# A depthwise convolution of 31 taps as 256 small matmuls with Toeplitz tap matrices

## The chip, the core and the metric

The kernel runs on one core of a Trainium2 chip. The core has five engines with a queue each: TensorE (PE, matmuls; its weight loads stand as PEld), VectorE (DVE), ScalarE (ACT), GpSimd (POOL) and SyncE (SP), which here issues the DMAs. A DMA is carried by up to 16 DMA engines. The metric is the device time of one execution in microseconds (us).

## The reference

Two encoder layers over 1024 tokens of width 1024. In each, one input projection feeds four token mixers of 256 columns; their outputs go through an output projection, then a residual layer norm, a SwiGLU feed-forward part and another residual layer norm. The mixers are a conformer convolution, a bidirectional S5 state space layer, a short gated convolution and differential attention. The change is about the first:

```
def conformer_conv(h, dw_w, dw_b, ln_g, ln_b):
    a, g = jnp.split(h, 2, axis=-1)
    z = a * jax.nn.sigmoid(g)
    z = depthwise_conv(z, dw_w) + dw_b      # 31 taps, centred, one filter per channel
    z = layer_norm(z, ln_g, ln_b)
    return jax.nn.silu(z)
```

So each of 256 channels is convolved along the 1024 tokens with its own 31 weights. Everything is float32.

## The kernel before

**Precision.** A wide product of the projections is done as three matmuls of split operands (high and low parts, in a reduced fp32 format, `mm3`): tiles `cg` (`chan_gemm`, channels on partitions), `tg` (`tok_gemm`, tokens on partitions), `up` and `dn` (feed-forward), `wo`. Transposes go through PE as plain fp32 matmuls against an identity (`tr`); such an fp32 matmul shows as two records in the trace.

**Order of the work.** The program is written stage by stage (`mixers_in`, attention, feed-forward), but a `Weaver` records every operation, with a modelled duration, and then builds one static order for all engines by list scheduling. The priority of an operation is its place in the program plus an offset from the table `SHIFT`, by function and layer; operations that may run on several engines are placed with the help of the table `PREF`. All instructions are emitted from one helper, so every line of the profile says L461, and tile names tell them apart. On the chip each engine follows its list strictly: an instruction that waits holds all behind it on its engine, and SP's DMA issues are such a list too.

**A layer.** `load_small` brings the small vectors (31 tap rows, biases, gains) into `chraw` (38 rows x 256), PE transposes them (`chps`) to channel-major `chp`. In layer 0 `s5_params` loads the S5 parameters into `s5b`, transposes them (`s5ps`, `s5cps`) and computes tables on DVE. `conf_a` and `conf_g` form z = a x sigmoid(g) in tile `conv`. The S5 layer runs as eight pairs of groups: `s5_pair_tables` builds tables (tiles `s5t`, in a ring of four, and `s5k`), `s5_pair` does matmuls (`s5v`, `s5y`, `s5wp`) and vector operations between them on DVE and POOL. The short convolution's products stand between the pairs.

**The convolution.** `conf_conv` works with channels on partitions, for each of two channel tiles. Even and odd tokens are separated; with sums and differences of them the 31 taps take 46 `scalar_tensor_tensor` operations of some 505 columns and one `tensor_scalar`, all on DVE, each reading and writing the PSUM tile `cacc`, so they form a chain:

```
dst[:, lo:hi] = src[:, lo+k:hi+k] * weight(k) + dst[:, lo:hi]
```

Then ACT copies `cacc` to `acc`, PE transposes that to tokens on partitions (`cvt`, 16 per layer), DVE takes mean and variance (`bn_stats`) and normalises into `cxn`, PE transposes back (`cvb`, 16), and ACT applies gain, bias and Silu and hands the result to the output projection by way of DRAM (`yT`). After that come the products for attention (`ktp`, `tg`) and the attention heads, whose first score tile is `sc`.

Of the kernel before, what the change touches and what calls it, by code (L numbers as in the profile page):

```python
# [9 lines left out]
F32 = mybir.dt.float32  # L10
# [8 lines left out]
P = 128  # L19
# [26 lines left out]
R_CW, R_SW, R_CB, R_LG, R_LB, R_GB, NROW, NCH = 0, 31, 34, 35, 36, 37, 38, 54  # L46
# [16 lines left out]
class Weaver:  # L63
# [3 lines left out]
    SHIFT = {"None": 315, "attn_finish0": 3482, "attn_finish1": -8000, "attn_heads0": 4301, "attn_heads1": 1337,  # L67
# [11 lines left out]
    PREF = {"attn_finish0 gpsimd": -5172, "attn_finish0 scalar": -2719, "attn_finish0 vector": -2311,  # L79
# [106 lines left out]
    def record(self, eng, method, args, kwargs):  # L186
# [104 lines left out]

    LAT = {"tensor": 200.0, "vector": 140.0, "scalar": 160.0, "gpsimd": 120.0, "sync": 100.0}

    def schedule(self):
# [44 lines left out]
        while True:  # L339
# [104 lines left out]
            for x in o.succ:  # L444
                x.left -= 1
                x.ready = max(x.ready, o.end + (0.0 if e == x.eng == "tensor" else self.LAT[e]))
                if x.left == 0:
                    offer(x)
# [26 lines left out]
class Trunk:  # L475
# [3 lines left out]
    def __init__(self, ctx, tc, t):  # L479
# [17 lines left out]
        self.mhalf = self.cp.tile([P, 4], F32, name="mhalf")  # L497
# [59 lines left out]
    def layer_norm(self, r, g, bb, dst=None, parts=1):  # L557

        nc = self.nc
        st = self.sp.tile([P, 2, 6], F32, tag="st", name=self.nm("st"))  # L560
# [79 lines left out]
    def load_small(self, l):  # L640
        nc, t = self.nc, self.t
        raw = self.wb([NROW, GW], "chraw")
        nc.sync.dma_start(raw[R_CW:R_CW + CONV_K, :], t["conf_dw_w"][l])
        nc.sync.dma_start(raw[R_SW:R_SW + 3, :], t["sc_conv_w"][l])
        for r, k in ((R_CB, "conf_dw_b"), (R_LG, "conf_ln_g"), (R_LB, "conf_ln_b"), (R_GB, "s5_b_glu")):
            nc.sync.dma_start(raw[r:r + 1, :], t[k][l:l + 1, :])
        ch = self.cp.tile([P, 2, NCH], F32, tag="chp", name=self.nm("chp"), bufs=1)
# [192 lines left out]
    def s5_ring(self):  # L840

        tabs = [self.S([P, SROW], F32, "s5t") for _ in range(2)]
        wk = self.S([P, SROW], F32, "s5k")
        self.s5t, self.s5w = [], []
        for i in range(4):
            T = tabs[i // 2][:, (i % 2) * 1856:(i % 2) * 1856 + 1856]
# [12 lines left out]
        self.s5BD = tabs[0][:, 3712:3904].rearrange("p (r g m) -> p r g m", r=2, g=2)  # L859
# [3 lines left out]
    def s5_pair_tables(self, pr):  # L863
# [3 lines left out]
        R, G = self.s5t[pr % 4], self.s5p  # L867
# [143 lines left out]
    def conv_alloc(self):  # L1011
        T = self.S([P, 2, 2, NJ, P], F32, "conv")
# [660 lines left out]
```

## Time and profile before

| | |
|---|---|
| median of three runs | 2543.04 us (2540.66 to 2545.26) |
| the profiled execution | 2556.47 us, span 2554.3 us, mean granted TensorE clock 0.959 |
| PE busy | 2342.5 us, 92% of the span |
| DVE busy | 1690.8 us, 66% |
| ACT, POOL busy | 777.7 us (30%), 1383.9 us (54%) |

The page gives busy times over the whole span; they are sums over stages with different limits. The stages, found from the first and last instructions of certain tiles, are: layer 0's mixers up to the first score tile at 350 us, its attention to 624, its feed-forward part to 1307; layer 1's mixers to 1607, attention to 1876, feed-forward to 2489, and the last norm. A wait's row names the instruction that waited, the one that ended the wait, the total, how often, and the longest. The granted clock is a share of 2.4 GHz: 0.5 is 1.2 GHz.

### The profile page before, as it was taken

The page shows a single profiled execution, that of the slowest core. Times are in us where ns is not written, and L with a number is a line of the kernel's source. Part 1 is how long each engine was busy: PE and PEld are TensorE (multiplying, and loading weights), DVE is VectorE, ACT ScalarE, POOL GpSimd, SP SyncE. Part 2 cuts the span into 40 slices and gives each one's busy share as a digit, 9 for nine tenths or more (in the row PEclk, how much of TensorE's full clock was granted, in tenths as well). Part 3 has the DMA queues.
Part 4 walks back from the last instruction along what each step waited for, and adds up shares of the span by engine and source line. Part 5 has one row for each costly group of instructions (what it writes and reads, how often), then busy time and mean ns, then how long its engine had stood idle before and what let it go on. Part 6 is the DMA issues. An engine that isn't in the chain of part 4 may idle for free. (4 is left out here: it accounts for less than half of the span.)

```text
span 2554.3 us, 32493 instructions
## 1 busy us (share of the span) xinstructions
PE 2342.5 (92%) x12412; PEld 1941.9 (76%) x12412; DVE 1690.8 (66%) x2584; ACT 777.7 (30%) x1333; POOL 1383.9 (54%) x1162
## 2 busy tenths in 40 slices
PE   7798698888999999999999996898889999999997
PEld 7677586776888788888787785777678888888885
DVE  6789867886555555555668897688755444554456
ACT  2210245553222222222222111656433222222231
POOL 1524364546666555566675252644476655555574
PEclk9998798999999999999999997999999999999998
DMA  5212111114111111111322121211131111111112
GB/s 134 77 36 75 42 58 61 62 58 145 56 50 50 51 57 58 50 50 50 108 94 60 30 96 41 73 63 60 65 132 53 55 58 50 58 50 50 58 50 99
DMA packets 126439, 167.59 MB, mean 66 GB/s; under 512 B 18432, under 2 KB 100940, under 8 KB 126028
## 3 DMA queue, kind: packets, MB, share of 16 engines
q1 hardware_dynamic: 126284, 165.52, 20.5%
q8 instruction: 98, 1.61, 0.3%
q14 instruction: 57, 0.47, 0.1%
HBM read 139.25 MB, written 26.25 MB: 65 GB/s over the span
## 5 line engine op out<-in xcount | busy, mean ns | idle before, releaser
L461 PE MATMUL up<-xT,wring 128*128 128x512 f32 x2112 | 485.9, 389 | 0.0
L461 PEld LDWEIGHTS up<-xT,wring 128*128 128x128 f32 x2112 | 396.4, 188 | 82.3
L461 PE MATMUL dn<-wring,g 128*128 128x512 f32 x1920 | 451.0, 391 | 7.8 <-POOL wring L461 6.5
L461 POOL TENSOR_TENSOR wring<-upraw,wring 128x512 fp32r<-128x512 f32 x220 | 307.6, 1401 | 257.1 <-ACT wring L461 255.0
L461 PEld LDWEIGHTS dn<-wring,g 128*128 128x128 f32 x1920 | 359.3, 188 | 88.2 <-POOL wring L461 10.6
L461 PE MATMUL up<-xB,wring 128*128 128x512 f32 x1584 | 371.8, 390 | 0.0
L461 PEld LDWEIGHTS up<-xB,wring 128*128 128x128 f32 x1584 | 298.4, 189 | 62.2 <-DVE xT L461 0.2
L461 DVE TENSOR_TENSOR r<-r,dn 128x512 f32<-128x512 f32 x288 | 197.5, 686 | 212.0 <-PE dn L461 212.0
L461 ACT CAST wring<-upraw 128x512 fp32r<-128x512 f32 x217 | 134.6, 621 | 459.1 <-PE dn L461 164.8
L461 PE MATMUL cg<-xh,win 128*128 128x512 f32 x640 | 211.7, 400 | 4.6 <-POOL win L461 3.2
L461 DVE TENSOR_REDUCE asm<-sc 128x1 f32<-128x1024 f32 x128 | 155.3, 1217 | 65.9 <-PE sc L461 64.8
L461 PE MATMUL tg<-win,xh 128*128 128x256 f32 x1024 | 196.4, 291 | 1.4 <-ACT vq L461 0.9
L461 PE MATMUL wo<-wout,yhl 128*128 128x512 f32 x768 | 195.7, 402 | 0.0
L461 PEld LDWEIGHTS tg<-win,xh 128*128 128x128 f32 x1024 | 165.6, 197 | 4.1 <-ACT vq L461 1.3
L461 ACT ACTIVATE probs<-sc,asm 128x1024 f32<-128x1024 f32 x128 | 143.6, 1123 | 82.1 <-DVE asm L461 81.9
L461 PEld LDWEIGHTS wo<-wout,yhl 128*128 128x128 f32 x768 | 143.5, 192 | 28.9
L461 POOL TENSOR_TENSOR wring<-w2raw,wring 128x512 fp32r<-128x512 f32 x80 | 102.7, 1288 | 106.5 <-ACT wring L461 106.4
L461 PE MATMUL tg<-win,xl 128*128 128x256 f32 x512 | 148.8, 291 | 0.0
L461 PEld LDWEIGHTS cg<-xh,win 128*128 128x128 f32 x640 | 121.0, 189 | 35.1 <-issue 4.6
L461 POOL TENSOR_TENSOR wring<-tw,wring 128x512 fp32r<-128x512 f32 x88 | 126.2, 1434 | 13.2 <-ACT wring L461 13.2
L461 PE MATMUL cg<-xl,win 128*128 128x512 f32 x320 | 125.5, 392 | 0.0
L461 DVE TENSOR_TENSOR tw<-tu,up 128x512 f32<-128x512 f32 x66 | 45.4, 687 | 107.5 <-PE up L461 107.2
(234 smaller groups left out, 3856.9 us busy)
## 6 DMA issues: line engine op xcount, KB each, us to landing
upraw<-in_w_ffn_dram SPq DMA_DIRECT2D x88, 512.0 KB
w2raw<-in_w_ffn_dram SPq DMA_DIRECT2D x44, 512.0 KB
wraw<-in_w_in_dram SPq DMA_DIRECT2D x36, 512.0 KB
woraw<-in_w_out_dram SPq DMA_DIRECT2D x16, 512.0 KB
r<-x_scr SPq DMA_DIRECT2D x16, 512.0 KB
x_scr<-xr SPq DMA_DIRECT2D x14, 512.0 KB
yt<-yT_scr SPq DMA_DIRECT2D x16, 384.0 KB
x1row<-x_scr SPq DMA_DIRECT2D x12, 512.0 KB
```

What stands on the lines that cost most here:

```text
L461: getattr(e, method)(*args, **kwargs)
```

## The change

The tap loops on DVE are replaced by matmuls. For a block of 96 outputs of one channel, a window of 128 inputs is needed (96 + 31 - 1, with padding). A 128 x 96 matrix that holds the channel's taps along its diagonals maps the window to the outputs. The 1024 tokens are cut into 11 such blocks, so the moving operand has 11 columns, one per block, and there is one matmul per channel: 256 per layer, plain fp32.

- `conv_table`, once at the start: the taps of both layers go into the zeroed tile `ctw`, are halved by POOL and written to a DRAM table `taps_scr`, in which each row serves nine channels. Two transfers write zeros at both ends of the rows (58 x 864 values) and two, one per layer, write the taps between, 31 x 29 runs of nine values.
- `conv_windows`: 22 transposes per layer (`cvw`) bring the padded z to windows with tokens on partitions (`convz`).
- `conv_part`, three per layer, placed ahead of S5 pairs 0, 3 and 6: for every nine channels one DMA reads a 128 x 864 tile from the table with overlapping rows (29 per layer, in a ring of three: `ctap` twice and a part of tile `conv`), then nine matmuls into PSUM tile `cvo`; six evacuations on DVE per layer add the bias.
- `conv_norm`: mean and variance over 96-token blocks, normalisation, 22 transposes `cvb` of 96 columns, Silu.

Beside it `load_small` no longer loads the taps (`chraw` has 6 rows), the S5 table ring has two tiles instead of four, `conf_g` computes tanh in place in PSUM, two small pools have one buffer less, the scheduler's model has a higher floor for fp32 matmuls (128 ns) and an extra 75 ns for results that go to PE, and all numbers of `SHIFT` and `PREF` are new, so that the whole order moves. The core of the diff:

```diff
-    SHIFT = {"None": 315, "attn_finish0": 3482, "attn_finish1": -8000, "attn_heads0": 4301, "attn_heads1": 1337,
...
+    SHIFT = {"None": -921, "attn_finish0": -1102, "attn_finish1": -4137, "attn_heads0": 3121, "attn_heads1": -3970,
...
-            return max(108.0, 0.4167 * 4 * n + 5) * (0.57 if pair else 1.0), 0
+            return max(128.0, 0.4167 * 4 * n + 5) * (0.57 if pair else 1.0), 0
...
+    def conv_table(self):
+
+        nc, t = self.nc, self.t
+        self.wrd = self.dp.tile([DEPTH * NCK, WROW], F32, name="taps_scr")
+        w = self.wb([P, CB * CG], "ctw")
+        nc.gpsimd.memset(w, 0.0)
+        taps = w[64:64 + CONV_K, 0:DEPTH * NCK * CG].rearrange("p (l c) -> p l c", l=DEPTH)
+        for l in range(DEPTH):
+            nc.sync.dma_start(taps[:, l, 0:GW], t["conf_dw_w"][l])
+
+        nc.gpsimd.tensor_scalar(taps, taps, 0.5, None, op0=ALU.mult)
+        lo, hi = CB * CG, (CWIN - 1) * CG
+        nc.sync.dma_start(self.wrd[:, 0:lo], w[0:DEPTH * NCK, :])
+        nc.sync.dma_start(self.wrd[:, hi:WROW], w[0:DEPTH * NCK, :])
+        for l in range(DEPTH):
+            nc.sync.dma_start(self.wrd[l * NCK:(l + 1) * NCK, lo:hi].rearrange("q (i k) -> i q k", k=CG),
+                              taps[:, l].rearrange("p (q k) -> p q k", k=CG))
...
-    def conf_conv(self, l, yT):
...
-            v.tensor_scalar(acc[:, 1], w, cw(NROW + 8), cw(R_CB), op0=ALU.mult, op1=ALU.add)
-            taps(acc[:, 1], w, lambda k: cw(NROW + 8 + k), None, [k for k in range(-8, 8) if k], H)
...
-            taps(acc[:, 0], e, lambda k: cw(R_CW + 15 + 2 * k), acc[:, 1], [0] + [k for k in range(-7, 8) if k], H)
-            taps(acc[:, 1], zf, lambda k: cw(R_CW + 14 + 2 * k), None, range(-7, 9), H + 1)
...
+    def conv_part(self, l, i):
+
+        nc = self.nc
+        ps = self.d((P, 2, 512), "cvo")
+        for h in range(2):
+            b = 2 * i + h
+            c0, c1 = b * CBANK, min(GW, b * CBANK + CBANK)
+            for c in range(c0, c1):
+                q, k = divmod(c, CG)
+                tap = self.tring[q % 3]
+                if k == 0:
+                    src = self.wrd[l * NCK + q:l * NCK + q + 1, :]
+                    nc.sync.dma_start(tap, bass.AP(src.tensor, src.offset, [[CG, CWIN], [1, CB * CG]]))
+                nc.tensor.matmul(ps[0:CB, h, (c - c0) * NBLK:(c - c0 + 1) * NBLK], lhsT=tap[:, k::CG], rhs=self.zT[:, :, c], start=True, stop=True)
+            nc.vector.tensor_tensor(self.zT[0:CB, :, c0:c1].rearrange("p b c -> p c b"),
+                                    ps[0:CB, h, 0:(c1 - c0) * NBLK].rearrange("p (c b) -> p c b", b=NBLK),
+                                    self.cbias[:, c0:c1].unsqueeze(2).to_broadcast([CB, c1 - c0, NBLK]), op=ALU.add)
...
+            if pr % 3 == 0:
+                self.conv_part(l, pr // 3)
             self.s5_pair(pr)
...
+        self.conv_norm(l, yT)
...
+        self.conv_table()
```

Where it moves the order, at three places. First SP's list near the program's start (`x` are the input tiles, `wraw` weight blocks), before:

```order
L461 DMA lam_287<-in_da_subln_g_dram 64x1 x2
L461 DMA lam_1253<-in_da_subln_g_dram 64x1
L461 DMA x_3_83<-in_x_dram 128x1024 x4
L461 DMA lam_1253<-in_da_subln_g_dram 64x1
L461 DMA wraw_108<-in_w_in_dram 128x4x256
L461 DMA wraw_109<-in_w_in_dram 128x4x256
L461 DMA s5b_124<-in_s_a_re_dram 16x2x64
L461 DMA s5b_124<-in_s_a_im_dram 16x2x64
```

and now:

```order
L470 DMA taps_scr<-ctw_89 31x29x9 x2
L470 DMA wraw_110<-in_w_in_dram 128x4x256
L470 DMA wraw_111<-in_w_in_dram 128x4x256
L470 DMA ctap_53_134<-taps_scr 128x864
L470 DMA ctap_54_135<-taps_scr 128x864
L470 DMA chraw_117<-in_sc_conv_w_dram 3x256
L470 DMA chraw_117<-in_conf_ln_g_dram 1x256
L470 DMA chraw_117<-in_conf_ln_b_dram 1x256
L470 DMA chraw_117<-in_s_b_glu_dram 1x256
L470 DMA conv_120<-taps_scr 128x864
L470 DMA s5b_126<-in_s_a_re_dram 16x2x64
```

The two taps transfers and the first three reads of the table stand between the last input tiles and the S5 parameters; `chraw` comes behind the table too.

Second, PE's list where the small vectors and S5 parameters are transposed, before:

```order
L461 MATMUL chps_117<-ident,chraw_115 128x38 x2
L461 MATMUL tg_112<-win_88,xl_6_86 128x256
L461 MATMUL tg_112<-win_88,xh_4_84 128x256 x2
L461 MATMUL tg_112<-win_88,xl_6_86 128x256
L461 MATMUL s5ps_125<-ident,s5b_124 128x16 x3
L461 MATMUL s5ps_125<-ident,s5b_124 16x16
L461 MATMUL s5ps_126<-ident,s5b_124 128x16 x3
L461 MATMUL s5ps_126<-ident,s5b_124 16x16
```

and now:

```order
L470 MATMUL tg_114<-win_90,xl_6_86 128x256
L470 MATMUL tg_114<-win_90,xh_4_84 128x256 x2
L470 MATMUL tg_114<-win_90,xl_6_86 128x256
L470 MATMUL tg_114<-win_90,xh_4_84 128x256
L470 MATMUL s5ps_127<-ident,s5b_126 128x16 x3
L470 MATMUL s5ps_127<-ident,s5b_126 16x16
L470 MATMUL tg_114<-win_90,xh_4_84 128x256
```

Now `chps` stands nine rows ahead of `s5ps`. Ahead of `s5ps` PE had 96 `tg` matmuls before and has 70 now, and the same 64 transposes of `x`.

Third, PE's list in layer 0 at the first S5 pair, where the taps are now (three ring tiles, nine matmuls each):

```order
L470 MATMUL cg_174<-xh_4_84,win_91 128x512
L470 MATMUL cvw_162<-ident,conv_120 128x128 x3
L470 MATMUL s5v_164<-s5u_112,s5t_144 64x128 x8
L470 MATMUL cvo_163<-convz_133,ctap_53_134 96x11 x9
L470 MATMUL cvo_163<-convz_133,ctap_54_135 96x11 x9
L470 MATMUL cvo_163<-convz_133,conv_120 96x11 x9
L470 MATMUL cg_175<-xh_4_84,win_91 128x512
L470 MATMUL cg_175<-xl_6_86,win_91 128x512
L470 MATMUL cg_175<-xh_4_84,win_91 128x512 x2
```

and PE's transposes of the convolution in layer 0, before:

```order
L461 MATMUL tg_275<-win_89,xl_6_86 128x256
L461 MATMUL cvt_218<-ident,acc_213 128x128
L461 MATMUL cvt_218<-ident,acc_214 128x128
L461 MATMUL cvt_218<-ident,acc_213 128x128
L461 MATMUL cvt_218<-ident,acc_214 128x128
L461 MATMUL cvt_223<-ident,acc_213 128x128
L461 MATMUL cvt_223<-ident,acc_214 128x128
L461 MATMUL cvt_223<-ident,acc_213 128x128
L461 MATMUL cvt_223<-ident,acc_214 128x128
L461 MATMUL cvb_228<-ident,cxn_217 128x128 x4
L461 MATMUL cvb_229<-ident,cxn_217 128x128 x4
```

and now:

```order
L470 MATMUL tg_262<-win_91,xl_6_86 128x256
L470 MATMUL tg_262<-win_91,xh_4_84 128x256
L470 MATMUL s5gl_223<-s5u_112,wglu_216 128x512 x2
L470 MATMUL s5gl_224<-s5u_112,wglu_216 128x512 x2
L470 MATMUL cvb_225<-ident,convz_133 128x96 x5
L470 MATMUL tg_262<-win_91,xh_4_84 128x256
L470 MATMUL tg_262<-win_91,xl_6_86 128x256
L470 MATMUL tg_262<-win_91,xh_4_84 128x256 x2
```

The old transposes stood in one piece behind the last `tg` products of their block; the new ones stand in groups of five among such products.

## Rows read from the trace of the kernel before

**Rows 1.** stages: busy us of PE, PEld, DVE, ACT, POOL; clock, DMA share, GB/s.
```profile
87.00:245.00 158.00, 129.94 (x693) 105.30 (x692) 141.22 (x277) 21.28 (x44) 63.29 (x58) 0.89 0.21 56
245.00:350.00 105.00, 82.01 (x582) 73.91 (x581) 80.89 (x138) 23.02 (x36) 41.45 (x60) 0.82 0.15 50
1336.00:1496.00 160.00, 148.45 (x825) 121.38 (x825) 139.17 (x279) 28.06 (x53) 73.08 (x66) 0.99 0.22 58
1496.00:1607.00 111.00, 87.18 (x624) 79.04 (x624) 81.08 (x139) 26.63 (x41) 48.58 (x65) 0.85 0.17 57
```

**Rows 2.** PE's waits, 87 to 245 us: line, releaser, us in total, times, longest.
```profile
PE s5wp L461 <- DVE s5k L461: 16.9, 8, 6.8
```

**Rows 3.** PE's waits, 285 to 350 us, then 1500 to 1607.
```profile
PE cvt L461 <- ACT acc L461: 16.9, 2, 15.4
PE cvb L461 <- DVE cxn L461: 4.9, 2, 2.5
...
PE cvt L461 <- ACT acc L461: 17.1, 2, 15.6
PE cvb L461 <- DVE cxn L461: 5.2, 2, 2.7
```

**Rows 4.** instructions on tile `cacc`: ns min/median/max; then a window of them.
```profile
L461 DVE SCALAR_TENSOR_TENSOR cacc<-conv,chp,cacc x124: 735/749/756, 229.2 to 1555.7; 128x505 f32<-128x505 f32 x16, 128x506 f32<-128x506 f32 x16, 128x507 f32<-128x507 f32 x16, 128x508 f32<-128x508 f32 x16
L461 DVE SCALAR_TENSOR_TENSOR cacc<-acc,chp,cacc x60: 735/752/756, 252.3 to 1552.7; 128x505 f32<-128x505 f32 x8, 128x506 f32<-128x506 f32 x8, 128x507 f32<-128x507 f32 x8, 128x508 f32<-128x508 f32 x8
L461 DVE TENSOR_SCALAR cacc<-conv,chp x4: 799/806/811, 228.4 to 1481.3; 128x512 f32<-128x512 f32 x4
...
87.00:245.00 158.00, 11.54 (x17) 0.00 (x0) 0.89 0.21 56
```

**Rows 5.** windows of low granted clock.
```profile
42.10:52.40 10.30, 9.06 (x59) 9.05 (x60) 10.20 (x76) 1.35 (x3) 0.46 (x2) 0.50 0.01 2
291.00:329.00 38.00, 17.99 (x83) 14.14 (x84) 27.94 (x55) 9.01 (x13) 8.39 (x12) 0.51 0.12 39
```

**Rows 6.** PE's timeline: start, us, operation; then weight loads: busy us, mean ns.
```profile
33.05 0.59 PE L461 MATMUL s5ps<-ident,s5b 16*128 16x16 f32 x8
35.07 1.93 PE L461 MATMUL s5cps<-ident,s5b 16*128 16x16 f32 x32
43.34 3.16 PE L461 MATMUL s5cps<-ident,s5b 16*128 16x16 f32 x32 [3.51 <-DMA s5b<-in_s_c_re_dram]
...
L461 PEld LDWEIGHTS cvt<-ident,acc 128*128 128x128 f32 x32 | 5.8, 215 | 36.2 <-ACT acc L461 35.2 <-ACT conv L461 0.8
L461 PEld LDWEIGHTS cvb<-ident,cxn 128*128 128x128 f32 x32 | 5.5, 207 | 13.4 <-issue 11.4 <-DVE cxn L461 2.0
```

**Rows 7.** S5 operations by shape: ns min/median/max, on DVE and GpSimd (POOL).
```profile
L461 DVE TENSOR_TENSOR s5k<-s5k x47: 403/426/1749, 111.4 to 1477.8; 64x254 f32<-64x254 f32 x36, 128x256 f32<-128x256 f32 x11
...
L461 POOL TENSOR_TENSOR s5k<-s5k x49: 712/787/2432, 106.5 to 1476.5; 64x254 f32<-64x254 f32 x28, 128x256 f32<-128x256 f32 x21
...
L461 POOL TENSOR_TENSOR s5t<-P x38: 618/710/3443, 89.3 to 1371.1; 128x256 f32<-128x256 f32 x19, 128x288 f32<-128x288 f32 x19
```

**Rows 8.** DMA at 8:11, and GB/s in 40 slices of 11:12.7.
```profile
DMA packets 1041, 1.06 MB, mean 353 GB/s; under 512 B 37, under 2 KB 1031, under 8 KB 1041
...
GB/s 217 169 73 72 72 24 48 48 48 48 48 48 48 48 48 48 24 0 24 24 24 24 24 24 24 24 24 24 24 25 25 0 24 25 25 25 25 25 0 1
```

**Rows 9.** DMA queue, 27 to 30 and 93.4 to 94.3: packets, MB, share.
```profile
q1 hardware_dynamic: 3521, 0.22, 75.9%
...
q1 hardware_dynamic: 144, 0.07, 50.1%
```

**Rows 10.** SP's timeline of issues.
```profile
4.14 0.59 SPq L461 DMA_DIRECT2D chraw<-in_conf_dw_w_dram  x1
...
17.31 0.90 SPq L461 DMA_DIRECT2D s5b<-in_s_a_re_dram  x1
...
25.32 0.50 SPq L461 DMA_DIRECT2D s5b<-in_s_d_dram  x1
```

More of the change, by code (lines that the diff above doesn't have):

```diff
@@ L43 @@
 LN2_LO = -2.12194440e-4
-R_CW, R_SW, R_CB, R_LG, R_LB, R_GB, NROW, NCH = 0, 31, 34, 35, 36, 37, 38, 54
+R_SW, R_LG, R_LB, R_GB, NROW = 0, 3, 4, 5, 6
+CB, CWIN, NBLK, CG = 96, 128, 11, 9
+NCK = -(-GW // CG)
+WROW = (CB + CWIN - 1) * CG
+CBANK = 43
 class Rec:
@@ L445, in schedule @@
                 x.left -= 1
-                x.ready = max(x.ready, o.end + (0.0 if e == x.eng == "tensor" else self.LAT[e]))
+                x.ready = max(x.ready, o.end + (0.0 if e == x.eng == "tensor" else self.LAT[e] + (self.TOPE if x.eng == "tensor" else 0.0)))
                 if x.left == 0:
@@ L496, in __init__ @@
         self.ident = self.identr.bitcast(F32)
-        self.mhalf = self.cp.tile([P, 4], F32, name="mhalf")
+        self.mhalf = self.cp.tile([P, 6], F32, name="mhalf")
         nc.vector.memset(self.mhalf, -0.5)
@@ L559, in layer_norm @@
         nc = self.nc
-        st = self.sp.tile([P, 2, 6], F32, tag="st", name=self.nm("st"))
+        st = self.sp.tile([P, 2, 6], F32, tag="st", name=self.nm("st"), bufs=2)
         mv = self.sp.tile([P, 2], F32, tag="mv", name=self.nm("mv"))
@@ L642, in load_small @@
         raw = self.wb([NROW, GW], "chraw")
-        nc.sync.dma_start(raw[R_CW:R_CW + CONV_K, :], t["conf_dw_w"][l])
         nc.sync.dma_start(raw[R_SW:R_SW + 3, :], t["sc_conv_w"][l])
-        for r, k in ((R_CB, "conf_dw_b"), (R_LG, "conf_ln_g"), (R_LB, "conf_ln_b"), (R_GB, "s5_b_glu")):
+        for r, k in ((R_LG, "conf_ln_g"), (R_LB, "conf_ln_b"), (R_GB, "s5_b_glu")):
             nc.sync.dma_start(raw[r:r + 1, :], t[k][l:l + 1, :])
-        ch = self.cp.tile([P, 2, NCH], F32, tag="chp", name=self.nm("chp"), bufs=1)
+        ch = self.cp.tile([P, 2, NROW], F32, tag="chp", name=self.nm("chp"), bufs=1)
         ps = self.b((P, 2, NROW), "chps")
@@ L840, in s5_ring @@
     def s5_ring(self):
-        tabs = [self.S([P, SROW], F32, "s5t") for _ in range(2)]
+        tabs = self.S([P, SROW], F32, "s5t")
         wk = self.S([P, SROW], F32, "s5k")
         self.s5t, self.s5w = [], []
-        for i in range(4):
-            T = tabs[i // 2][:, (i % 2) * 1856:(i % 2) * 1856 + 1856]
+        for i in range(2):
+            T = tabs[:, i * 1856:i * 1856 + 1856]
             self.s5t.append(dict(
@@ L1011, in conv_alloc, with conv_alloc2 @@
     def conv_alloc(self):
-        T = self.S([P, 2, 2, NJ, P], F32, "conv")
-        self.p = [T[:, 1, c] for c in range(2)]
-        self.z = [T[:, 0, c].rearrange("p j s -> p (j s)").rearrange("p (t n) -> p t n", t=2) for c in range(2)]
-    def z_half(self, ct, hf):
-        return self.z[ct].rearrange("p t (c h i) -> p h i t c", h=2, i=2)[:, hf]
+        T = self.convt = self.S([P, SROW], F32, "conv")
+        self.zp = [T[:, c * 1088:c * 1088 + 1088] for c in range(2)]
+        for z in self.zp:
+            self.nc.gpsimd.memset(z[:, 0:16], 0.0)
+            self.nc.gpsimd.memset(z[:, 16 + SEQ:], 0.0)
+    def z_half(self, ct, hf):
+        return self.zp[ct][:, 16:16 + SEQ].rearrange("p (c j) -> p j c", j=NJ)[:, 4 * hf:4 * hf + 4]
+    def conv_alloc2(self):
+        T, T2 = self.convt, self.S([P, SROW], F32, "convz")
+        n = NBLK * GW
+        self.p = [t.rearrange("p (j s) -> p j s", s=P) for t in (T[:, 2176:3200], T2[:, n:n + 1024])]
+        self.zT = T2[:, 0:n].rearrange("p (b c) -> p b c", c=GW)
+        self.cst = T2[0:CB, n + 1024:]
+        self.tring = [self.wa([P, CB * CG], f"ctap{i}") for i in range(2)] + [T[:, 3200:3200 + CB * CG]]
+    @step
+    def conv_table(self):
[13 more added lines that the diff above has]
+                              taps[:, l].rearrange("p (q k) -> p q k", k=CG))
     @step
@@ L1023, in conf_a @@
         ps = self.chan_gemm(xT, w, ct, hf)
-        self.nc.scalar.copy(self.z_half(ct, hf), ps.rearrange("p (i t s) -> p i t s", t=2, s=P))
+        self.nc.scalar.copy(self.z_half(ct, hf), ps.rearrange("p (j s) -> p j s", s=P))
     @step
@@ new lines, in conv_windows @@
+    def conv_windows(self, l):
+        nc = self.nc
+        self.cbias = self.cp.tile([CB, GW], F32, tag="cbias", name=self.nm("cbias"), bufs=1)
+        nc.sync.dma_start(self.cbias, self.t["conf_dw_b"][l:l + 1, :].to_broadcast([CB, GW]))
+        for b0 in range(0, NBLK, 4):
+            n = min(4, NBLK - b0)
+            for ct in range(2):
+                ps = self.b((P, 4, P), "cvw")
+                for i in range(n):
+                    c0 = (b0 + i) * CB
+                    self.tr(ps[:, i, :], self.zp[ct][:, c0:c0 + CWIN])
+                nc.scalar.copy(self.zT[:, b0:b0 + n, ct * P:ct * P + P], ps[:, 0:n])
@@ new lines, in conv_part @@
+    @step
+    def conv_part(self, l, i):
+        nc = self.nc
+        ps = self.d((P, 2, 512), "cvo")
[12 more added lines that the diff above has]
+                                    self.cbias[:, c0:c1].unsqueeze(2).to_broadcast([CB, c1 - c0, NBLK]), op=ALU.add)
@@ new lines, in conv_norm @@
+    @step
+    def conv_norm(self, l, yT):
+        nc, ch = self.nc, self.ch
+        y = self.zT[0:CB]
+        st = self.cst[:, 0:66].rearrange("p (b n) -> p b n", n=6)
+        mv = self.cst[:, 66:88].rearrange("p (b n) -> p b n", n=2)
+        out = [z[:, 0:SEQ].rearrange("p (j c) -> p j c", j=NJ) for z in self.zp]
+        rs, nb = self.cst[:, 88:99], self.cst[:, 99:110]
+        for b0, b1 in ((0, 5), (5, 11)):
+            for b in range(b0, b1):
+                nc.vector.bn_stats(st[:, b, :], y[:, b, :])
+                nc.vector.bn_aggr(mv[:, b, :], st[:, b, :])
+            r, n = rs[:, b0:b1], nb[:, b0:b1]
+            nc.gpsimd.tensor_scalar(r, mv[:, b0:b1, 1], EPS, None, op0=ALU.add)
+            nc.gpsimd.tensor_tensor(r, r, self.mhalf[0:CB, 0:b1 - b0], op=ALU.pow)
+            nc.vector.scalar_tensor_tensor(n, mv[:, b0:b1, 0], -1.0, r, op0=ALU.mult, op1=ALU.mult)
+            for b in range(b0, b1):
+                nc.any3.affine(y[:, b, :], y[:, b, :], rs[:, b:b + 1], nb[:, b:b + 1])
+            for a0 in range(b0, b1, 5):
+                a1 = min(a0 + 5, b1)
+                m = min(SEQ, a1 * CB) - a0 * CB
+                for ct in range(2):
+                    ps = self.b((P, 512), "cvb")
+                    for b in range(a0, a1):
+                        nc.tensor.transpose(ps[:, (b - a0) * CB:(b - a0 + 1) * CB], y[:, b, ct * P:ct * P + P], self.ident[0:CB, CB - 1::-1])
+                    c0 = a0 * CB // NJ
+                    nc.scalar.activation(out[ct][:, :, c0:c0 + m // NJ].rearrange("p j c -> p c j"),
+                                         ps[:, 0:m].rearrange("p (c j) -> p c j", j=NJ), AF.Silu,
+                                         scale=ch[:, ct, R_LG:R_LG + 1], bias=ch[:, ct, R_LB:R_LB + 1])
+        for ct in range(2):
+            nc.sync.dma_start(yT[ct].rearrange("p (j c) -> p j c", j=NJ), out[ct])
```

76 lines of the change are left out of this document (14 added, 62 removed), and 60 rows, old and new, of tables (PREF, SHIFT).

## Prediction

> **What bounds the kernel now.** I read the busy times by stage first [rows 1], then what TensorE (PE) waits for in the stages that the change touches [rows 2, 3], then the tap loops themselves [rows 4], and last the start of the program, where the change puts new transfers [rows 6, 8 to 10]. PE is busy 92% of the span by the page's first part, so what counts is where it is not. [Rows 1] has the four stretches of interest: in layer 0 the stretch with the S5 chain (87 to 245 us) and the one from there to the first attention scores (245 to 350); in layer 1 the same two (1336 to 1496, 1496 to 1607). PE lacks 158 - 130 = 28 us in the first and 105 - 82 = 23 in the second, 11.5 and 24 in layer 1.
>
> Two causes stand behind this. In 87 to 245 VectorE (DVE) is busy 141 of 158 us and PE waits for its S5 results [rows 2]: 16.9 us for `s5wp` alone. This stretch is bound by the DVE chain, with PE beside it not full. In the two later stretches PE waits for the conformer convolution: 16.9 us for `acc`, the copy of the finished taps, and 4.9 for `cxn` in layer 0, 17.1 and 5.2 in layer 1 [rows 3]. The taps run behind the S5 chain because DVE has no room before it. While PE idles there its granted clock falls to 0.51 of full speed, 1.2 GHz instead of 2.4, from 291 to 329 us [rows 5]; over the whole stretch it is 0.82, and 0.85 in layer 1's [rows 1].
>
> **What goes.** The taps are 124 instructions at about 0.749 us, 60 at 0.752 and 4 at 0.806 [rows 4], 124 x 0.749 + 60 x 0.752 + 4 x 0.806 = 141 us, nearly 70 per layer of DVE. What the path loses is the wait, not the sum: 16.9 + 4.9 = 21.8 us in layer 0, 22.3 in layer 1. With the wait goes the low clock behind it: PE did 18.0 us of work at half speed in layer 0 [rows 5], half of which comes back, 9 us; the clock that layer 1 lacks is 0.15 x 111 = 17 us beside 0.18 x 105 = 19, so 8 there. In the new order the convolution's last transposes `cvb` stand among `tg` products, so the normalisation on DVE and ScalarE has cover; without that cover a wait of some us like the one for `cxn` stays.
>
> **What comes on PE.** Per layer 256 fp32 tap matmuls, 96 columns of weights and 11 moving columns each, 22 transposes `cvw`, and 22 narrower `cvb` for 16 `cvt` and 16 `cvb`. An fp32 matmul is two records in the trace. The nearest row is `s5cps`: small matmuls of 16 columns, each with its own weight load, 32 records in 1.93 us at 35 us, 60 ns each, and 32 in 3.16 us, 99 ns, at 43 us where the granted clock was 0.50 [rows 5, 6]. So the taps are 512 x 60 ns = 31 us, or 51 at half clock, per layer. They load their weights with a stride of nine values; the old `cvt` read its tile with a stride of four and its loads took 215 ns, beside 207 for `cvb` without one [rows 6], so I give the stride nothing. The transposes are 28 more less 16, at 0.11 us about 1.3 us. I take 32 us per layer; the bounds are 32 and 52.
>
> The Trainium skill, "TensorE: Matmul & The Clock Gate", section "LDWEIGHTS (loading the stationary operand)", puts a load at its columns divided by 1.2, so 80 ns for 96 columns; two loads to a tap matmul would make 41 us per layer in place of 31. The trace's `s5cps` pairs with 128 columns come every 60 ns, and the measurement decides.
>
> **What hides it.** In layer 0 the tap matmuls stand in the S5 stretch, between `cg` products and S5 steps, where PE lacks 28 us; in layer 1 11.5. That is cover as long as DVE stays the bound there. DVE gets back the 11.5 us of taps that it did there [rows 4], and takes six evacuations per layer (the nearest row is the 128x512 start of a tap loop at 0.806 us, so 5 us). It also takes nearly all the S5 operations of GpSimd: 49 and 38 in the two costliest groups [rows 7], 44 per layer at the 0.43 us that such an operation takes on DVE, 19 us. That is 141 - 11.5 + 5 + 19 = 153.5 of 158 us at most, so DVE is full but not late. So I take the whole 28 and 11.5 as used, which is the favourable end; the other end is none, if the order's guesses place the taps where a result is awaited anyway.
>
> Layer 1 then is 32 - 22.3 - 8 - 11.5 = -10 us, and layer 0, but for the start, 32 - 21.8 - 9 - 28 = -27.
>
> **The start.** Here stands the cost that the diff does not show. `conv_table` writes the taps to a DRAM table in two transfers of 31 x 29 runs of 36 bytes, 899 each. The trace shows what a transfer with 31 rows does: behind the other loads `chraw` with its 31 rows of 1 KB runs at a flat 24 GB/s, one engine's share of the 353 that all 16 moved just before [rows 8]. So 1798 runs go through one DMA engine. The nearest row for a small run is the S5 load: 3521 packets (64 bytes) kept 16 engines 75.9% busy for 3 us [rows 9], 3 x 16 x 0.759 / 3521 = 10.3 ns. At about 11 ns the table takes 20 us. Ahead of it stand 8 `x` tiles and two weight tiles, 5.2 MB, 15 us at 353 GB/s, and on this engine alone the raw taps and half of the zero fills, 62 and 200 KB, 11 us at 24 GB/s: I let the table begin at 15 + 11 = 26 us and end at 46.
>
> The Trainium skill, "DMA: Bandwidth & Descriptors", section "Why a DMA increments its semaphore by 16 and not by 1", says that a transfer takes the largest number of engines up to 16 that divides its slowest dimension on both sides; 31 has no such divisor but one. The trace agrees with the 24 GB/s.
>
> Who waits for it? SP's queue is in order, and the tap loads `ctap`, which read the table, now stand ahead of `chraw` and of every S5 parameter load `s5b`, which were issued at 4.1 and from 17.3 us before [rows 10]. PE has the transposes of both, `chps` and `s5ps`, at a place in its order where it cannot pass them, and the DVE chain begins with them. From the first `s5b` issue to `s5ps` it took 33.05 - 17.31 = 16 us; some of that was PE's own work, the loads take about 10 (17.31 to 25.32, and 2 to land). With `chraw` that puts `s5ps` at about 46 + 13 = 59 us, not 33. Three us of PE work move behind it (26 `tg` products fewer stand ahead), so PE loses 59 - 33 + 3 = 29 us more. Layer 0 is thus 29 - 27 = +2.
>
> **The sum.** +2 - 10 = -8 us. Attention, FFN and the tail are re-ordered too, with the same products; I give them nothing, with 10 us either way. The profiled execution took 2556.5 us (span 2554.3), 13 over the median, and -8 on the median gives 2535 us.
>
> **Rivals.** (1) The table costs more. The trace shows no small writes to DRAM; the nearest are `m_scr` runs of 512 bytes: 144 packets at 50.1% of 16 engines in 0.9 us, 50 ns each [rows 9]. At that price the table takes 90 us, `s5ps` comes 70 us later again, and the time is about 2605. Each ns per run is worth 1.8 us, so this decides the sign from about 15 ns on; at 25 ns the time is 2560. For it speaks that writes of 512 bytes, twenty times the data at a rate far below that of reads, are all that is seen of this kind; against it that those ran on 16 engines at once into one small region, and these come one at a time. In the Trainium skill, "DMA: Bandwidth & Descriptors", section "Specifications", runs under 512 bytes are said to make the engine read, modify and write; no run here shows what that costs at 36 bytes.
>
> (2) The taps run at the low clock. They move 11 columns per load, and `s5cps` at half clock took 99 ns a record. If each group pulled the granted clock to 0.5, two layers cost 40 us more: 2575. Against it: the groups stand between wide `cg` products, and at 35 us 32 records ran at the full price. Half of the groups would be 2555.
>
> (3) More is gained. If the table costs nothing on the path (-27 in layer 0) and layer 1 stays as summed, it is 2543 - 37 = 2506. For it speaks that DVE loses 70 us a layer and that the S5 chain, which PE waits for [rows 2], loses its hand-overs to GpSimd, whose operations take 0.79 us to DVE's 0.43 [rows 7]; against it that `s5b` does stand behind the table.
>
> (4) No change: PE is the bound at 92%, 65 us of matmuls come, and what waited is filled by just that much: 2543, give or take 5.
>
> **Chances.** Forecast (2512 to 2538) 0.36; (3), below it, 0.15; (4) 0.15; (1) 0.23; (2) 0.11. What can be told from no change is about 0.2%, 5 us; so faster 0.51, same 0.15, slower 0.34. The forecast's own range is 2512 to 2538; to hold 8 in 10 the range runs from 2498, where (3) and a better attention order meet, to 2590, a table at some 42 ns a run.
>
> **What would show it.** `s5ps` of PE near 59 us: earlier and the table is cheap, beyond 75 and rival 1 holds. No wait of PE on `acc` or `cxn`, and the clock near 1.0 from the last S5 step to the first scores. `cvo` at about 60 ns a record; near 99 with a PEclk of 0.5 means rival 2. First scores at about 352 us in layer 0, and 290 us after the first `tg` in layer 1, where it took 299.5. If attention or FFN move by over 10 us each, the sum is wrong where I gave nothing.

## The result, and the profile after

The changed kernel takes 2677.55 us (median of four, 2672.28 to 2679.16) where the kernel before took 2544.15: 1.0519 times as long, with a 95% interval of 1.0496 to 1.0543. The forecast was 8 us less; it is 133 us more, outside the range. The profiled execution has a span of 2677.4 us. One execution, of 5355 us, of the version with a new table and 44 columns, stands far outside all others and is left out of its median.

The span falls into the same stages as before. Their borders are the first instructions of certain tiles on PE, read from the timelines of the two kernels:

| stage | before, us | after, us | difference |
|---|---|---|---|
| start to first `sc` (layer 0's mixers) | 349.9 | 433.7 | +83.8 |
| to first `up` (attention) | 274.4 | 258.5 | -15.9 |
| to first `tg` of layer 1 (feed-forward) | 683.2 | 674.7 | -8.5 |
| to first `sc` (layer 1's mixers) | 299.5 | 367.6 | +68.1 |
| to first `up` (attention) | 265.9 | 255.5 | -10.4 |
| to the end | 681.4 | 687.4 | +6.0 |

So everything was lost in the mixers, 152 us, and 29 came back elsewhere. The busy times of the two stretches in which the tap matmuls stand (columns as in [rows 1]) show PE full and its clock low; behind the taps, up to the first scores, it is high:

```profile
148.70:363.40 214.70, 211.67 (x1127) 193.46 (x1125) 126.46 (x274) 13.83 (x30) 20.87 (x11) 0.76 0.28 87
1451.30:1665.40 214.10, 211.52 (x1163) 193.37 (x1163) 121.27 (x281) 15.53 (x33) 5.61 (x5) 0.77 0.28 88
...
363.40:433.70 70.30, 69.34 (x551) 65.11 (x552) 21.46 (x61) 31.67 (x51) 42.30 (x57) 0.98 0.21 69
1665.40:1734.50 69.10, 68.42 (x532) 64.03 (x533) 20.11 (x52) 33.64 (x56) 41.70 (x59) 0.96 0.20 69
```

Of 214.7 us PE is busy 211.7, where in the S5 stretch before it lacked 28 of 158; the granted clock is 0.76 and 0.77, where the S5 stretches before had 0.89 and 0.99 [rows 1]. The weight loads of the tap matmuls (ns least/median/most):

```profile
L470 PEld LDWEIGHTS cvo<-convz,ctap x700: 253/277/283, 148.7 to 1665.4; 128*96 128x96 f32 x175
```

One load of 96 columns takes 277 ns, longer than the 215 and 207 of the old transposes' 128 columns at the low clock [rows 6]; its least is 253. Loads overlap, so the pace is another thing. How far apart the records come is seen in the timeline of PE at the first group:

```profile
148.65 6.65 PE L470 MATMUL cvo<-convz,ctap 128*96 128x11 f32 x36
155.15 3.39 PE L470 MATMUL cvo<-convz,conv 128*96 128x11 f32 x18
158.38 0.77 PE L470 MATMUL cg<-xh,win 128*128 128x512 f32 x1
158.96 0.63 PE L470 MATMUL cg<-xl,win 128*128 128x512 f32 x1
...
162.40 0.39 PE L470 MATMUL cg<-xl,win 128*128 128x512 f32 x1
```

36 records in 6.65 us and 18 in 3.39 are 185 and 188 ns each; from start to start the median is 180 ns in every bank of both layers, whether the granted clock is high or low. From start to start the 512 records of a layer add up to 91 us, where 31 were forecast. Behind them the first `cg` products take 0.63 us instead of 0.39: the clock is at the lower level there, and from 162.4 us on they take 0.39 again.

The start came out near the prediction. SP's issues, PE's longest wait up to 150 us, and the DMA queue from 38.4 to 50 us:

```profile
20.14 18.24 SPq L470 DMA_DIRECT2D taps_scr<-ctw  x2
38.48 11.99 SPq L470 DMA_DIRECT2D wraw<-in_w_in_dram  x2
50.56 0.92 SPq L470 DMA_DIRECT2D ctap<-taps_scr  x2
...
55.28 0.33 SPq L470 DMA_DIRECT2D s5b<-in_s_a_re_dram  x1
```
```profile
PE chps L470 <- DVE xl L470: 20.9, 1, 20.9
```
```profile
q1 hardware_dynamic: 896, 0.03, 11.8%
```

In 11.6 us 896 runs moved, one every 13 ns, while nothing else did; all 1798 took from 28.7 to 51.1 us. SP itself was held meanwhile: it stood 17.9 us at the issue of the second transfer and 11.4 us at that of the first weight block behind it. PE stands at `chps` for 20.9 us. The releaser named, `xl`, ended 0.06 us before `chps` began; on DVE it stood behind the cast of a weight block, and that waited for a load issued behind the table:

```profile
55.29 2.68 DVE L470 CAST win<-wraw 128x1024 fp32r<-128x1024 f32 x1 [20.04 <-DMA wraw<-in_w_in_dram]
57.89 0.67 DVE L470 TENSOR_TENSOR xl<-xtp,xh 128x512 fp32r<-128x512 f32 x1
```

The load of `chraw`, behind the table too, had been seen by PE at 58.1 us, half a microsecond earlier. `s5ps` comes at 61.6 us. And the convolution's old waits on `acc` and `cxn` are gone, in both layers. PE's longest waits from 245 to 434 us are:

```profile
PE s5wp L470 <- DVE s5k L470: 0.7, 1, 0.7
PE ktp L470 <- ACT kst L470: 0.7, 1, 0.7
```

### The profile page after: what moved, and what is told of

It reads as the page before. It is cut to its first block, busy times and chain, and to the rows that moved or that the text cites. A ratio compares the mean times of both kernels' runs of the same rounds, so it can differ in the third digit from the quotient of the medians.

```text
span 2677.4 us, 34449 instructions
## 1 busy us (share of the span) xinstructions
PE 2535.7 (95%) x13460; PEld 2146.3 (80%) x13460; DVE 1591.7 (59%) x2538; ACT 786.8 (29%) x1339; POOL 1284.4 (48%) x1040
## 5 line engine op out<-in xcount | busy, mean ns | idle before, releaser
L470 POOL CAST win<-wraw 128x1024 fp32r<-128x1024 f32 x23 | 32.7, 1425 | 413.3 <-PE cg L470 345.8
L470 PE MATMUL cg<-xh,win 128*128 128x512 f32 x640 | 227.6, 426 | 2.3 <-ACT conv L470 0.8
L470 PE MATMUL tg<-win,xh 128*128 128x256 f32 x1024 | 206.1, 300 | 0.4 <-DVE sca L470 0.4
L470 PEld LDWEIGHTS tg<-win,xh 128*128 128x128 f32 x1024 | 173.4, 206 | 2.3 <-DVE sca L470 0.8
L470 PEld LDWEIGHTS cg<-xh,win 128*128 128x128 f32 x640 | 131.2, 205 | 34.7 <-issue 3.2
L470 PE MATMUL tg<-win,xl 128*128 128x256 f32 x512 | 155.1, 303 | 0.0
L470 PE MATMUL cg<-xl,win 128*128 128x512 f32 x320 | 133.7, 418 | 0.0
L470 PEld LDWEIGHTS cvo<-convz,ctap 128*96 128x96 f32 x700 | 128.9, 277 | 1.6 <-issue 1.1
```

Of the source, the lines that this page charges most:

```text
L470: getattr(e, method)(*args, **kwargs)
```

## The experiments

Theory A: the tap matmul takes its weights with a stride of nine values (36 bytes), and loading them so costs 180 ns a record instead of 60. Theory B: the cost is the low clock that a stretch of matmuls with 11 columns brings. Theory C: the late table and the new order.

**Contiguous weights.** One edit of the changed kernel:

```diff
-lhsT=tap[:, k::CG]
+lhsT=tap[:, k * CB:(k + 1) * CB]
```

> The changed kernel with one edit: each tap matmul takes its 96 weight columns from 96 neighbouring values of the tap tile, not from every ninth (so it multiplies by the wrong taps; work, order and DMAs are the same). Theory A (the weight load with a stride of nine values is slow): the pairs of cvo come every 60 to 80 ns instead of 185, weight loads near 140 ns instead of 277, and 1024 x (0.185 - 0.060) = 128 us go if nothing hides them: 2677 - 128 = about 2550 us, 2575 if a part was hidden. Theory B (the granted clock falls because tap matmuls stream 11 columns only, and that is the cost): the columns stay 11, the records stay near 185 ns, the time within 10 us of 2677. Theory C (the late table and the new order lost it): within 10 us of 2677.

Measured: 2583.62 us, 94 less; ratio to the kernel before 1.0153 (1.0124 to 1.0181). The load's row and the first groups in the timeline:

```profile
L470 PEld LDWEIGHTS cvo<-convz,ctap x700: 159/165/285, 146.5 to 1571.1; 128*96 128x96 f32 x175
```
```profile
146.53 3.23 PE L470 MATMUL cvo<-convz,ctap 128*96 128x11 f32 x36
149.61 2.78 PE L470 MATMUL cvo<-convz,conv 128*96 128x11 f32 x18
152.23 0.77 PE L470 MATMUL cg<-xh,win 128*128 128x512 f32 x1
```

Theory A holds in kind: 3.23 us for 36 records, 90 ns each; the median from start to start is 85 ns. But the next 18 take 2.78, 154 ns each, and the `cg` product behind them 0.77: that is the clock. 410 of 512 records in layer 0 are under 100 ns and 96 above 140; together they take 51 us, so 40 per layer went with the stride and 20 of the forecast's miss stayed. That the time fell by 94 us, not by 128, was a miss of theory A's size (85 to 90 ns, not 60), and 39 us remain to explain.

**The stride by itself.** The same line with another stride for each bank of 43 channels:

```diff
+ST = ((1, 2, 3, 4, 5, 6), (7, 8, 9, 1, 2, 4))
-lhsT=tap[:, k::CG]
+lhsT=tap[:, k:k + ST[l][b] * (CB - 1) + 1:ST[l][b]]
```

> The changed kernel with another weight stride in each of the twelve banks of 43 channels: 1, 2, 3, 4, 5, 6 values in layer 0, and 7, 8, 9, 1, 2, 4 in layer 1 (wrong taps again, all else the same). Theory A: the time per cvo record grows with the stride, 60 to 80 ns at 1 and 185 at 9, and the old transposes with a stride of 4 say that 4 is still cheap or nearly so (under 120). Theory B: all banks near 185 ns, whatever the stride, apart from the clock. Theory C: says nothing of it.

Measured: 2637.8 us (one run). A row of the timeline for each of the strides 1 to 6, in order:

```profile
148.20 3.23 PE L470 MATMUL cvo<-convz,ctap 128*96 128x11 f32 x36
...
163.21 1.76 PE L470 MATMUL cvo<-convz,conv 128*96 128x11 f32 x18
...
230.03 2.42 PE L470 MATMUL cvo<-convz,conv 128*96 128x11 f32 x18
...
286.27 3.22 PE L470 MATMUL cvo<-convz,conv 128*96 128x11 f32 x18
...
314.82 3.17 PE L470 MATMUL cvo<-convz,ctap 128*96 128x11 f32 x18
...
327.56 3.05 PE L470 MATMUL cvo<-convz,ctap 128*96 128x11 f32 x18
```

By these rows that is 90, 98, 134, 179, 176 and 169 ns a record, the end of each group's last record included. From start to start the medians at full clock are 85, 89, 132, 176, 167 and 168 ns for strides 1 to 6, and 173, 180 and 180 for 7, 8 and 9 in layer 1, whose banks with 1, 2 and 4 agree (85, 90, 176). At half clock strides 1, 2 and 3 take 160 ns, and from 4 on the times are those of full clock. So the cost rises up to a stride of four values (16 bytes) and then stays, and half clock hides most of it. Theory A holds, but "4 is still cheap" was wrong: the old `cvt`, which I took as the witness that a stride costs nothing, is a transpose and says nothing of these matmuls (see the part on why). The Trainium skill, "SBUF — State Buffer", section "Door 1: The DMA port swizzle (why `[64,N]` ≈ `[32,N]`)", says in a note that SBUF is read in lines of 16 bytes, that two hits on a line are needed for full rate, and that a crossing to a new line costs. The plateau from 16 bytes on and the small price at 8, where two values share a line, agree; that one could step four fp32 values for free, as the note has it, does not agree with 176 ns.

**The table by itself.** Stride of nine kept; the two transfers of 899 runs are replaced by two of 29 runs:

```diff
-nc.sync.dma_start(self.wrd[l * NCK:(l + 1) * NCK, lo:hi].rearrange("q (i k) -> i q k", k=CG),
-                  taps[:, l].rearrange("p (q k) -> p q k", k=CG))
+nc.sync.dma_start(self.wrd[l * NCK:(l + 1) * NCK, lo:hi], w[64:64 + NCK, 0:hi - lo])
```

> The changed kernel, stride of nine kept, but the two transfers of 899 runs of 36 bytes are replaced by two of 29 runs of 1116 bytes of the same size (the table then holds the taps in the wrong places). Start term of the prediction: s5ps comes near 40 us instead of 61.6, since 22 us of one DMA engine go; if nothing behind it takes that up, the time falls by 20 to 25 us to about 2655. Theory A alone, with layer 0 bound by the tap matmuls on PE and not by the chain from the S5 parameters: PE still waits for chps, so it falls too, by 15 to 25. If the wait was hidden: within 5 us of 2677.

Measured: 2655.73 us, 22 less than the changed kernel; ratio to before 1.044 (1.0414 to 1.0466). The first and last `s5ps`:

```profile
L470 PE MATMUL s5ps<-ident,s5b x8: 171/208/231, 39.7 to 41.8; 16*128 16x16 f32 x6, 16*16 16x16 f32 x2
```

`s5ps` comes 21.9 us earlier and the end 21.8: nothing takes it up. SP's issues of the two transfers take 0.2 and 0.4 us here. The start term is shown, and of theory C the late table holds, for 22 of the 133 us.

**Both edits.**

> Both edits at once. Theory A with the start term: 2677 - 128 - 22 = about 2527 us, below the kernel before. If the two hide one another: 2540 to 2550. Theory B: about 2655, the start alone.

Measured: 2562.92 us, ratio 1.0069 (1.0052 to 1.0086); 20.7 below the contiguous run, so the two add up, but to 2563 and not to 2527. First `sc` is at 368.2 us, and layer 1's mixers take 316.4. The tap stretches of this kernel:

```profile
125.00:298.00 173.00, 169.41 (x1133) 152.21 (x1130) 126.44 (x275) 14.02 (x30) 20.84 (x11) 0.82 0.35 108
1387.00:1554.00 167.00, 164.45 (x1176) 147.50 (x1175) 123.38 (x283) 15.51 (x33) 5.52 (x5) 0.88 0.35 112
```

PE is full, and the clock is at 0.82 and 0.88. That leads to theory B for what remains.

**More columns.** The kernel with both edits, each tap matmul now with 44 moving columns:

```diff
-matmul(ps[0:CB, h, (c - c0) * NBLK:(c - c0 + 1) * NBLK], ..., rhs=self.zT[:, :, c])
+matmul(ps[0:CB, h, m * NBLK:(m + 4) * NBLK], ..., rhs=self.zT[:, :, n:n + 4] as (c b))   # m = min(c - c0, 39), n = min(c, 252)
```

> The run with contiguous weights and short table (2563 us), with 44 moving columns per tap matmul in place of 11 (results overwrite one another, so the output is wrong; count, weights and order are the same). If the granted clock falls in the tap stretches because little is streamed, it rises here: cvo records at 85 ns throughout instead of partly 160, their sum per layer 44 instead of 50 to 54 us, PEclk near 1.0 in the tap stretches, and 15 to 35 us less in all. If the clock falls for another reason: within 8 us of 2563. If the longer stream costs: 2575 and more.

Measured: 2521.78 us, ratio 0.9898 (0.988 to 0.9917): 41 us less, more than expected, with four times the columns. The two tap stretches, from the first to the last tap matmul, and the first groups:

```profile
127.20:276.50 149.30, 144.13 (x1131) 128.70 (x1128) 126.24 (x274) 13.85 (x30) 20.83 (x11) 0.98 0.40 125
1364.50:1515.40 150.90, 148.08 (x1167) 132.50 (x1166) 121.63 (x281) 15.54 (x33) 6.86 (x5) 0.98 0.39 124
```
```profile
127.26 3.27 PE L470 MATMUL cvo<-convz,ctap 128*96 128x44 f32 x36
130.35 1.71 PE L470 MATMUL cvo<-convz,conv 128*96 128x44 f32 x18
```

The record takes what it took at full clock, 91 to 95 ns by the rows and 85 from start to start, so the columns are free behind the weight load; what changed is the granted clock, 0.98 in both stretches. The records add up to 44 and 45 us per layer instead of 54 and 50, some 15 us in all. From the first tap matmul to the last, the two stretches are 38 us shorter together (149 and 151 us for 172 and 166), so the other 23 or so are the neighbours, at full clock now. Theory B is shown for this part.

**Half the tap matmuls.** One per two channels, 22 columns, the second channel's taps left out:

```diff
+if (c - c0) % 2 == 0:
+    n2 = min(2, c1 - c)
-    matmul(... NBLK], rhs=self.zT[:, :, c])
+    matmul(... (c - c0 + n2) * NBLK], rhs=self.zT[:, :, c:c + n2] as (c b))
```

> The run with contiguous weights and short table (2563 us), with one tap matmul for two channels (22 moving columns, the second channel's taps left out), so 128 instead of 256 per layer. If the tap matmuls stand on PE's path in full, 256 records of some 100 ns per layer go: about -50 us, to 2513. If half of their time lies in time that PE would wait anyway, as the prediction had it for layer 0 (28 us) and layer 1 (11.5): -10 to -25.

Measured: 2525.05 us, ratio 0.9914 (0.9898 to 0.993): 38 us less than with all. The records' sum fell from 54 to 27 us in layer 0 and from 50 to 24 in layer 1, 53 in all, so some 70% of what goes comes off the end. That is between the two forecasts and nearer to "in full". The clock changes with it (0.91 and 0.96 in the tap stretches), so it does not price the cover cleanly.

**The stride with more columns.** The changed kernel as it was, with 44 columns (written so that later channels overwrite, as below):

> The changed kernel as it was, stride of nine and late table, with 44 moving columns only (computes the reference). The weight load sets the record, so records stay at 180 ns, 91 us per layer. If the low clock beside the taps (PEclk 0.64 to 0.77 in the tap stretches) costs by itself, the neighbouring products get it back: 10 to 35 us less, 2643 to 2668. If the clock falls because PE waits for the slow loads, and not for the few columns: within 8 us of 2677.

Measured: 2668.36 us, ratio 1.0482 (1.0461 to 1.0502): 9 us less than without. The granted clock of the tap stretches rises only from 0.76 and 0.77 to 0.81 and 0.82:

```profile
148.70:363.00 214.30, 211.25 (x1141) 193.84 (x1141) 128.80 (x288) 12.94 (x30) 21.14 (x12) 0.81 0.28 88
1451.00:1665.00 214.00, 211.42 (x1184) 192.34 (x1184) 128.20 (x305) 21.15 (x42) 12.28 (x20) 0.82 0.27 86
```

That lies between the two forecasts: the columns help little while the loads are slow. The stride is the first cause, and most of the clock's part comes back only once it is gone.

**A table that needs no stride.** One DRAM row per channel, written from channel-major taps in runs of 124 bytes, 128 to a transfer, and read as 128 x 9 x 96; it computes the reference:

```diff
+self.wrd = self.dp.tile([DEPTH * GW, CB + CWIN - 1], F32, name="taps_scr")
+for g in range(4):
+    self.tr(ps[:, g, :], w[0:CONV_K, g * P:(g + 1) * P])
+...
+    nc.sync.dma_start(self.wrd[g * P:(g + 1) * P, CB:CWIN - 1], tv[:, g, :])
+...
+dma_start(tap as (k m), bass.AP(src.tensor, src.offset, [[1, CWIN], [CB + CWIN - 1, n], [1, CB]]))
```

> A whole version of the change with another table layout: one DRAM row of 223 values per channel, written from channel-major taps (four transposes on PE at the start, then 128 runs of 124 bytes per transfer), and read as 128 x 9 x 96, so that the 96 weight columns of a channel lie side by side. Computes the reference. If weight stride and the table's single DMA engine were the faults, it should stand near the run with both edits (2563): records of cvo near 85 ns, s5ps near 38 us, 2550 to 2565 us in all. If the layout of the reads (runs of 384 bytes) holds the tap matmuls up, PE waits for ctap and it is above 2575. That it beats the kernel before (2544) would need the low clock in the tap stretches to be gone, which neither edit touches.

Measured: 2566.44 us, ratio 1.0076 (1.0059 to 1.0094). `s5ps` is at 40.6 us, and PE waits for no tap load. It is just above the expected 2550 to 2565 us: the faults of layout are mended, and it is still slower than the tap loops.

**The same with 44 columns**, each later channel's matmul overwriting its own place, so that the reference is computed:

```diff
-ps[0:CB, h, (c - c0) * NBLK:(c - c0 + 1) * NBLK], ..., rhs=self.zT[:, :, c]
+ps[0:CB, h, (c - c0) * NBLK:(c - c0 + min(4, GW - c)) * NBLK], ..., rhs=self.zT[:, :, c:c + min(4, GW - c)] as (c b)
```

> The version with the per-channel table (2566 us) and 44 moving columns per tap matmul: channel c's matmul also writes the places of channels c+1 to c+3, and those channels' own matmuls overwrite them afterwards, so the reference is computed. If the granted clock in the tap stretches is what the wide columns gave back, it loses the same 41 us as the pair 2563 to 2522 did: about 2525 us, below the kernel before (2544 to 2548). If the gain of that pair came from its wrong data or another order: 2555 to 2570.

Measured: 2527.70 us (median of three), ratio 0.9927 (0.9908 to 0.9945), 39 us less than with 11 columns. It beats both kernels, the one before by 0.7%. The tap stretches are read from the next kernel, which differs in the table's place alone; its clock is high there:

```profile
129.90:281.00 151.10, 145.76 (x1127) 130.03 (x1126) 126.36 (x274) 13.82 (x30) 20.87 (x11) 0.97 0.46 121
1376.00:1527.00 151.00, 148.43 (x1168) 132.85 (x1167) 122.28 (x281) 15.79 (x34) 7.05 (x5) 0.98 0.46 123
```

**The table later.** As that, with the table's offset in `SHIFT` moved from -3371 to 2000:

> As the version with the per-channel table and 44 columns, with the table's place in the list moved behind the first input tiles (SHIFT of conv_table from -3371 to 2000). If the input tiles' delay at the start (first product at 18.9 us, 13.6 in the kernel before) is on the path: 3 to 6 us less than the version beside it. If PE waits for the S5 parameters anyway: within 3 us of it.

Measured: 2534.65 us, ratio 0.9955 (0.9937 to 0.9973). A miss: it is 7 us slower. The order put PE's transposes of the taps first all the same, so PE waits at once for the raw taps, which now come later; with the table at its old place and 11 columns that wait was 6.5 us in all:

```profile
PE ctps L470 <- DMA ctw<-in_conf_dw_w_dram: 15.4, 2, 14.4
```

**Old taps, new order.** The kernel before with the `SHIFT` and `PREF` entries of the changed one for attention, output projection, norms and layer 0's feed-forward part:

> The kernel before, tap loops and all, with the changed kernel's SHIFT and PREF entries for attention, output projection, norms and layer 0's feed-forward part alone. The changed kernel spent 16 and 10 us less in the attention of the two layers and 8 less in layer 0's feed-forward part. If these come from the order: about 2544 - 30 = 2514 us. If they come from what the convolution leaves behind (other work of the mixers that no longer reaches into attention): within 8 us of 2544.

Measured: 2531.33 us, ratio 0.994 (0.9922 to 0.9959). About 17 us of the expected 30 appear: attention takes 267.5 us in layer 0, between the 274.4 of before and the 258.5 of after, and layer 0's feed-forward part 673 instead of 683. So part of what the changed kernel gained outside the mixers is due to these tables alone, and with them the tap loops (2531) and the best tap matmuls that compute the reference (2528) come out alike. The rest of attention's gain may lie in other entries or in what the mixers leave to it; that was not tried.

## Why the prediction was wrong

The step that failed is the one on "What comes on PE": records of 60 ns, and "I give the stride nothing". A record takes 180 ns with the stride, at either clock, so a layer's taps take 91 us and not 31, or 51 as the upper bound had it. That is 60 us per layer, 120 in all; of the 120 ns that a record took more, 25 are the plain load of 96 columns (85 ns) and 95 the stride. In the profiled executions the mixers came out 160 us over the forecast (+152 for -8). The 40 us that the records leave are found by subtraction only; the clock and the start below bear on them. The stages that were given nothing gave 29 back, which leaves the 131 us between the span's change (+123) and the forecast; by the medians it is 141, since the profiled execution of the kernel before was 12 us over its median.

- *The witnesses were of another kind.* `s5cps`, `cvt` and `cvb` are transposes, and a transpose is one record in the trace, not two as the section on precision has it: 16 `cvt` per layer are 32 records [rows 6], where the 512 tap matmuls are 1024. `s5cps` (61 ns at full clock from start to start) has 16 rows and 128 columns in its weights and no stride; 85 ns is what the contiguous taps took for 128 rows and 96 columns. I set aside the Trainium skill, "TensorE: Matmul & The Clock Gate", section "LDWEIGHTS (loading the stationary operand)", whose 80 ns for 96 columns was nearer than my row; at half clock, though, the contiguous taps took 160.
- *`cvt` did not speak of the stride.* It read its tile with a stride of four and shows no price for it, beside `cvb` without one:

```profile
1560.96 2.27 PE L461 MATMUL cvb<-ident,cxn 128*128 128x128 f32 x8 [2.49 <-DVE cxn L461]
1563.24 1.69 PE L461 MATMUL cvt<-ident,acc 128*128 128x128 f32 x8
```

  Where they follow one another at half clock, the records of both come 213 ns apart; the one pair of `cvt` at full clock is 110 apart, as the transposes of `x` are without a stride (109). From the sweep's 176 ns for 96 columns, 128 would take 235 (an estimate). So the stride costs these transposes, of 128 moving columns, nothing that is seen, and the tap matmuls, of 11, all of it; which of the differences between them decides is not shown.
- *The clock* was to come back, 9 and 8 us. It did where it had been lost, to 0.98 and 0.96 behind the taps, and fell in a new place, to 0.76 and 0.77 in the tap stretches. Rival 2 named this, with its cause in the 11 columns; the pair with 11 and 44 columns bears it out at 41 us without the stride, and 9 with it. Its price was another: not records of 99 ns, since those with the stride take 180 at either clock, but slower neighbours.
- *The old waits* of PE for `acc` and `cxn` are gone, as forecast.
- *The start* was right in size: `s5ps` at 61.6 us for 59, a run every 13 ns for 11, and 22 us off the end when the runs are taken away. Rival 1's 50 ns a run is refuted (its 512 bytes are 14 times 36, not twenty times). That 11 came near 13 was in part luck: it was worked out from the time that packets take, and by the same working the runs of the table take 0.118 x 16 x 11.6 us / 896 = 24 ns and overlap. And what held SP was the issue of the transfers itself, before any reader of the table, while the last thing that PE waited for was the weight block behind it, with `chraw` half a microsecond ahead.
- *The cover*, in one sum with the other terms of the mixers, held. With the stride, the table and the clock out of the way the steps add up: in the run with 44 columns first `sc` is at 345.0 us. The forecast for layer 0 but for the start is 349.9 - 27 = 323; add 7 + 3 for `s5ps` at 39.7 instead of 33 with less work ahead of it, and 44 - 31 = 13 for the true price of the records, which gives 346. In layer 1, 299.5 - 10 + 14 = 303.5; measured 302.0. No run prices the cover by itself; and VectorE, which was summed to be full beside the taps, is busy 126 of the 149 us of layer 0's tap stretch in that run, PE 144.
- *What I gave nothing* was not nothing: attention -15.9 and -10.4, feed-forward -8.5 and +6.0, -29 in all, against a band of 10.

## What to carry to other kernels

Before work moves to TensorE as many small matmuls, price the weight load of one in its real layout: columns, stride, and records per matmul; here the stride alone doubled it, and 44 moving columns cost no more than 11. Lay the stationary operand out so that its columns are neighbours, in the DMA that brings it if need be. And read the price of an operation from rows of the same kind at the same clock: the transposes said nothing of the fp32 matmuls, and at half clock the tap loads took 160 ns without the stride and 180 with it, at full clock 85 and 180.

## What the runs showed of the hardware

- A weight load of 96 columns of an fp32 matmul sets a pace, at full clock, of 85 ns a record with neighbouring columns, 89 at a stride of 8 bytes, 132 at 12, 176 at 16, and 167 to 180 from 20 to 36. At half clock it is 160 up to 12 bytes, and the same as at full clock from 16 on.
- Transposes of 128 columns with a stride of 16 bytes (`cvt`) came 213 ns apart at half clock, as those without.
- 44 moving columns in place of 11 cost nothing behind such a load, and with neighbouring weights the granted clock of the stretch was 0.98 with the former, 0.82 and 0.88 with the latter: more work, and 41 us less. With the stride of 36 bytes it was 0.81 and 0.82 for 0.76 and 0.77, and 9 us less.
- 36-byte runs written to DRAM by a transfer with 31 rows followed one another every 13 ns. By the share of the queue a packet took 24 ns; by the same working the 64-byte reads took 10 and the 512-byte writes 50 [rows 9]. Behind the first transfer of 899 such runs, SP stood 17.9 us at the issue of the next, and then 11.4 us at that of a weight block; with 29 runs of 1116 bytes the two transfers took it 0.2 and 0.4 us.
